# A fused decoder layer on one core: x's first quarter on ScalarE's queue, the small rows transposed after the first sums, and places of stored factors given back five half steps later

## The chip, the cores and the metric

The kernel runs on 1 core of one Trainium2 chip. The metric is the device time of that core in microseconds (us), the median of the runs of a kernel; lower is better. The engines are named as the profile names them: PE (TensorE), DVE (VectorE), ACT (ScalarE), POOL (GpSimd) and SP (SyncE, which here only issues transfers). "SPq" and "ACTq" are the queues on which SP and ACT issue transfers; an engine works its instructions off in the order in which they stand, issues of transfers included.

## The reference

One layer: a modulated RMS norm, one wide input projection, eight heads of stick-breaking attention, eight heads of chunkwise retention, an output projection with a gate and a residual. S = 1024 rows, D = 2048, head width 128, all float32.

```python
mod = silu(c) @ w_ada + b_ada                 # -> shift, scale, gate, 2048 each
h   = rms_norm(x, norm_gain) * (1 + scale) + shift
proj = h @ w_in                               # 2048 -> 8192: q k v z | q k v z
oa  = stick_breaking_attention(rms_norm(q) , rms_norm(k), v) * silu(z)
ob  = head_group_norm(chunkwise_retention(rotary(q), rotary(k), v)) * silu(z)
y   = concat(oa, ob) @ w_out
out = x + gate * y
```

## The kernel before

**Products in three passes.** Each float32 operand is cut into a high part (ACT copies it to float32r) and a low part (DVE subtracts the high part); a product is then three matmuls, high by high, high by low, low by high (`mm3`, lines 190 to 192; the trace shows them as L190, L192 and L191). Cuts of weights are made by `split` into a pool of four high and four low buffers (tiles `wh`, `wl`), cuts of kept factors by `split_to` or by `high` and `low`.

**Stages.** In a first stage (lines 765 to 808) one eighth of the projection's columns is multiplied chunk by chunk for the first 512 rows of x: for each of 16 chunks `p` of D, x is transposed by PE (tiles `xtp`, copied to `xT`), the modulation for two chunks at a time is summed by PE from w_ada (tiles `ada`, sums `accp`, copied to `acc`, turned into columns as `mod`, and made into `mods` by DVE), `make_h` makes `h_hi` and `h_lo` out of `xT` and `mods`, and seven products per chunk (tiles `first`) run with the cut pieces `wh_first`, `wl_first` of the weight rows `wr`. The first of them needs `mods`, which needs the transposed table `cols` of the small rows (norm_gain, b_ada and the head gains), loaded by five small transfers into `rows`, transposed by PE (`rows_ps`) and copied by DVE. A second stage does the same for the other 512 rows and makes, a few pieces at a time, the right factors of what follows.

**The groups.** From then on the rest of the projection runs as seven products of a Strassen-like scheme per group of columns, in `ORDER1` = (2, 7, 4, 1, 6, 5, 3) for group 0. Their right factors are, in the order of `RIGHT`, B11, B21, B22, T4, T1, T2, T3, each of eight chunks k and two parts (`B21h`, `B21l` and so on). `B21`, `T3`, `T4`, `B11` (`FIXED`) stay in SBUF for group 0 and are stored to DRAM as they are used; `B22`, `T1`, `T2` are stored when made and loaded back later. An "entry" is one (group, product, half hh, column block q); it has twelve matmuls and two half steps: `tick()` is called after every second chunk, counts `clock`, and runs what `later(n, fn)` put off by n half steps and up to two pieces from the list `background`.

**Places.** All large tiles live in 92 places of 256 KB (`Slots`, 128 partitions by 512 words). `get` takes the place that has been free longest, `put` appends one to the list of the free ones. A `put` happens when the last use has been written into the program, not when that use has run: whoever gets the place waits on the chip for the last reader of the tile before, which for a stored factor is the transfer that stores it.

**What sets the order.** PE's instructions run in the order in which the code is written. Those of the other engines are ordered by a scheduler by priority; `tc.high_priority(AHEAD)` moves a block forward. Eight semaphores (DMAHW0 to DMAHW7) are given in turn to the transfers of both queues: a transfer that gets one again waits at its issue until the transfer eight before it has landed.

The lines that matter: `load_xq(0)` loads the first quarter of x's columns for row blocks 0 to 3 (four transfers of 256 KB), line 736; the small rows are loaded and transposed on lines 139 to 155; `low(n, k)` on line 619 makes the low part, stores both parts and gives both places back:

```python
            else:
                store(n, k, hi, lo)
                put(hi, lo)
```

Of the kernel before, what the change touches and what calls it, by code (L numbers as in the profile page):

```python
# [36 lines left out]
NW = 4  # L37
CLASSES = {"dst": 14, "raw": 24, "ring": 24, "att": 30}
XQ_LOAD = {0: 2, 4: 1, 8: 3}
XQ_STAT = {1: 0, 4: 2, 7: 1, 10: 3}  # L40
X_LOAD = {5: (4,), 7: (5,), 9: (6,), 11: (7,)}
X_STAT = {8: (4,), 10: (5,), 12: (6,), 13: (7,)}
BIAS_LEAD = 12
# [13 lines left out]
class Slots:  # L57
# [31 lines left out]
    def put(self, *tiles):  # L89
        for t in tiles:  # L90
            _, i, cls = self.of.pop(id(t))
            self.used[cls] -= 1
            self.free.append(i)
# [3 lines left out]
def layer_kernel(ctx, tc, x, c, w_ada, b_ada, norm_gain, w_in, sb_q_gain, sb_k_gain, ret_norm_gain, w_out,  # L97
# [33 lines left out]
    c_sb = cons.tile([P, 16], F32, name="c_sb")  # L131
    nc.scalar.dma_start(c_sb, c.rearrange("o (p j) -> (o p) j", j=16))
    kdec = cons.tile([P, NH], F32, name="kdec")

    silu_c = cons.tile([P, 16], F32, name="silu_c")
    nc.scalar.activation(silu_c, c_sb, AF.Sigmoid)
# [7 lines left out]
    nc.scalar.dma_start(rows[48:49, 0:P], sb_q_gain)  # L144
    nc.scalar.dma_start(rows[49:50, 0:P], sb_k_gain)
    nc.scalar.dma_start(rows[50:58, 0:P], ret_norm_gain.rearrange("o (k p) -> (o k) p", p=P))
    rows_ps = ps.tile([P, P], F32, tag="C", name="rows_ps")
    nc.tensor.transpose(rows_ps, rows[:, 0:P], ident)
    nc.vector.tensor_copy(cols, rows_ps[:, 0:58])
    put(rows)  # L150
    gain_c = cols[:, 0:16]
    shift_b = cols[:, 16:32]
    qkg = cons.tile([P, 1], F32, name="qkg")
    nc.vector.tensor_scalar(qkg, cols[:, 48:49], cols[:, 49:50], 1.0 / math.sqrt(HD), op0=ALU.mult, op1=ALU.mult)
    ret_g = cols[:, 50:58]

    def rsqrt_guess(y, m):
# [45 lines left out]
    def later(n, fn):  # L203
        due.setdefault(clock[0] + n, []).append(fn)
# [5 lines left out]
    def tick():  # L210
        clock[0] += 1
        for fn in due.pop(clock[0], ()):
            fn()
        pump()
        stepped = False
        for task in list(tasks):
            task[1] -= 1
            if task[1] > 0 or stepped and one_step[0]:
                continue
            stepped = True  # L220
            try:
                task[1] = next(task[0])
            except StopIteration:
                tasks.remove(task)
        if background and len(slots.free) >= 3:
            some(background, 2)
        next_sum()

# [268 lines left out]
    shift = cons.tile([P, KC], F32, name="shift")  # L497
    qb = cons.tile([P, 2, NH], F32, name="qb")
    nc.vector.memset(qb, 0.0)
    xt, ada, xT = {}, {}, {}  # L500

    def load_x(t):
        for qt in (0, 2, 1, 3):
# [3 lines left out]
    def load_ada(cc):  # L507

        col = (D + CHUNKS1[cc] * 2 * P) if cc < 8 else CHUNKS[cc - 8] * 2 * P
        for g in range(8):  # L510
            ada[cc, g] = ar = get(f"ada_{cc}_{g}")
            nc.sync.dma_start(ar.rearrange("p (j n) -> p j n", n=2 * P),
                              ada_rows[:, 2 * g:2 * g + 2, col:col + 2 * P])
# [67 lines left out]

    mods = cons.tile([P, KC], F32, name="mods")
    scale_b1 = cons.tile([P, KC], F32, name="scale_b1")
    nc.vector.tensor_scalar(scale_b1, cols[:, 32:48], 1.0, None, op0=ALU.add)

    def ada_mod(cc, acc):

# [30 lines left out]
    def low(n, k):  # L618
        def fn():
            src, hi = facs[n, k], facs.pop((n, k, "hi"))  # L620
            lo = get(f"{n}l_{k}", None, F32R, borrow=True)
            nc.vector.tensor_tensor(lo, src, hi.bitcast(F32), op=ALU.subtract)
            if n != "B21":
                put(facs.pop((n, k)))
            if n in FIXED:
                fixed[n, k] = hi, lo
            else:
                store(n, k, hi, lo)
                put(hi, lo)
        return fn  # L630

    def factors(ks):
# [129 lines left out]
        nc.vector.tensor_copy(row, tp)  # L762
        return row

    load_ada(0)
    load_xq(0)
    ws = {0: start_w(0, 0)}
    for p in range(2):
        x_turn(p, 0, "pj", 4)
    sums = {0: ada_sums(0)}  # L770
    ws[1] = start_w(1, 0)
    load_ada(1)
    with tc.high_priority(AHEAD):
        ada_mod(0, sums.pop(0))
        make_h(0, 0)
    make_h(1, 0)
    rawz = {}
    for p in range(KC):
# [1097 lines left out]
```

## Time and profile before

| what | us |
|---|---|
| median of 3 runs | 1894.58 (1893.50 to 1895.37) |
| the profiled execution, its own time | 1895.06 |
| its span in the profile | 1893.3 |
| PE busy in the span | 1866.6 (99%) |
| ACT busy | 831.4 (44%) |
| DVE busy | 1338.0 (71%) |
| moved by the transfer engines | 541.04 MB, 286 GB/s over the span |

The rest of the profile is shown with the prediction. A row of the timeline reads: start, duration, engine, line, operation, written tile, read tiles, shape, count, and in brackets the idle time of the engine before it with what ended it. Rows of PEld are the loads of weights that go with each matmul. The span is shorter than the execution's time by 1.76 us, and the profiled execution lies 0.48 us above the median.

### The profile page before, as it was taken

How to read it: one execution, taken by the hardware profiler on the slowest of the kernel's cores; microseconds unless marked ns; L12 is line 12 of the kernel's file. 1: busy time of each engine (PE TensorE's matmuls, PEld its weight loads, DVE VectorE, ACT ScalarE, POOL GpSimd, SP SyncE). 2: the span in 40 equal slices, each digit the busy share in tenths (PEclk: the TensorE clock that was granted, in tenths of full speed). 3: DMA queues.
4: the chain of work that ended last, by engine and by line, in shares of the span. 5: the costliest groups of instructions: out<-in, count | busy, mean ns of one | idle time of the engine just before them, and what ended most of it. 6: DMA issues, size and time to landing. Idle time of an engine off the chain costs nothing.

```text
span 1893.3 us, 28871 instructions
## 1 busy us (share of the span) xinstructions
PE 1866.6 (99%) x9515; PEld 1537.2 (81%) x9515; DVE 1338.0 (71%) x2598; ACT 831.4 (44%) x1559; POOL 81.9 (4%) x278
## 2 busy tenths in 40 slices
PE   7999999999999999999999999999999999999998
PEld 4777778888888888888888888888888888888887
DVE  2568775666768777776778686976686656596669
ACT  3647752224544454435543554334334455342231
POOL 0000000000100010001010101000000000000000
PEclk9999999999999999999999999999999999999999
DMA  9969999997798789978997989999997963994594
GB/s 332 354 207 317 315 334 374 377 357 263 235 299 303 244 286 297 303 274 287 292 320 265 302 277 307 294 303 288 299 341 247 270 211 111 371 364 149 183 316 162
DMA packets 411827, 541.04 MB, mean 286 GB/s; under 512 B 34078, under 2 KB 207512, under 8 KB 411676
## 3 DMA queue, kind: packets, MB, share of 16 engines
q1 hardware_dynamic: 411288, 539.02, 86.6%
q8 instruction: 75, 1.23, 0.3%
q14 instruction: 76, 0.62, 0.1%
q10 hardware_dynamic: 388, 0.17, 0.0%
HBM read 453.03 MB, written 86.02 MB: 285 GB/s over the span
## 4 chain that ended last, share of the span: by engine, by line
PE 90%; DVE 4%; DMA 4%; issue 1%; ACT 1%; SPq 0%; DVEq 0%; ACTq 0%
PE pj L190 19%; PE pj L192 19%; PE pj L191 18%; PE y L191 4%; PE y L190 4%; PE y L192 4%; PE first L190 3%; PE first L191 2%; PE first L192 2%; PE accp L575 2%; PE tp_B L1196 1%; PE oT L192 1%; PE oT L190 1%; PE oT L191 1%; PE zp L190 1%; PE zp L192 1%
## 5 line engine op out<-in xcount | busy, mean ns | idle before, releaser
L179 DVE TENSOR_TENSOR wl<-A,wh 128x512 fp32r<-128x512 f32 x392 | 270.0, 689 | 249.5 <-ACT wh L177 225.1
L177 ACT ACTIVATE wh<-A 128x512 fp32r<-128x512 f32 x392 | 246.7, 629 | 378.7 <-PE pj L191 357.7
L393 ACT ACTIVATE c<-pj 128x512 f32<-128x512 f32 x112 | 66.6, 598 | 162.3 <-PE pj L192 149.2
L396 DVE TENSOR_TENSOR c<-pj,c 128x512 f32<-128x512 f32 x112 | 74.9, 686 | 59.7 <-PE pj L192 59.5
L300 DVE TENSOR_TENSOR A<-A,A 128x512 f32<-128x512 f32 x160 | 109.3, 688 | 1.7
L190 PE MATMUL first<-h_hi,wh_first 128*128 128x512 f32 x224 | 94.5, 422 | 1.6 <-ACT h_hi L605 1.6
L1176 DVE TENSOR_TENSOR_SCAN om<-om 128x128 f32<-128x128 f32 (+2 forms) x96 | 93.3, 972 | 1.1
L190 PE MATMUL pj<-T1h,wh 128*128 128x512 f32 x232 | 92.6, 399 | 0.0
L190 PE MATMUL pj<-B22h,wh 128*128 128x512 f32 x232 | 92.3, 398 | 0.0
L190 PE MATMUL pj<-B21h,wh 128*128 128x512 f32 x232 | 92.2, 398 | 0.0
L190 PE MATMUL pj<-B11h,wh 128*128 128x512 f32 x232 | 91.9, 396 | 0.0
L192 PE MATMUL pj<-B21h,wl 128*128 128x512 f32 x232 | 90.8, 391 | 0.0
L192 PE MATMUL pj<-T1h,wl 128*128 128x512 f32 x232 | 90.8, 391 | 0.0
L191 PE MATMUL pj<-B21l,wh 128*128 128x512 f32 x232 | 90.6, 391 | 0.0
L192 PE MATMUL pj<-B22h,wl 128*128 128x512 f32 x232 | 90.6, 391 | 0.0
L191 PE MATMUL pj<-T1l,wh 128*128 128x512 f32 x232 | 90.6, 390 | 0.0
L192 PE MATMUL pj<-B11h,wl 128*128 128x512 f32 x232 | 90.5, 390 | 0.0
L191 PE MATMUL pj<-B11l,wh 128*128 128x512 f32 x232 | 90.4, 390 | 0.0
L191 PE MATMUL pj<-B22l,wh 128*128 128x512 f32 x232 | 90.4, 390 | 0.0
L192 PE MATMUL pj<-T3h,wl 128*128 128x512 f32 x224 | 88.1, 393 | 1.9 <-DVE wl L179 1.9
L190 PE MATMUL pj<-T3h,wh 128*128 128x512 f32 x224 | 88.7, 396 | 0.8 <-ACT wh L177 0.8
L190 PE MATMUL pj<-T4h,wh 128*128 128x512 f32 x224 | 89.3, 399 | 0.0
(400 smaller groups left out, 4930.6 us busy)
## 6 DMA issues: line engine op xcount, KB each, us to landing
A<-in_w_in_dram SPq DMA_DIRECT2D x228, 256.0 KB, 5.7
ada<-in_w_ada_dram SPq DMA_DIRECT2D x128, 256.0 KB, 5.6
wB<-in_w_out_dram SPq DMA_DIRECT2D x112, 256.0 KB, 5.3
gr<-in_w_ada_dram SPq DMA_DIRECT2D x64, 256.0 KB, 5.7
T2h<-fac_T SPq DMA_DIRECT2D x56, 256.0 KB, 5.2
T2l<-fac_T SPq DMA_DIRECT2D x56, 256.0 KB, 5.4
T1h<-fac_T SPq DMA_DIRECT2D x56, 256.0 KB, 5.4
T1l<-fac_T SPq DMA_DIRECT2D x56, 256.0 KB, 5.4
```

The lines of the kernel that those rows point to most:

```text
L177: nc.scalar.activation(hi[:, 0:n], src[:, 0:n], AF.Copy)
L179: nc.vector.tensor_tensor(lo[:, 0:n], src[:, 0:n], hi[:, 0:n].bitcast(F32), op=ALU.subtract)
L190: nc.tensor.matmul(o, a_hi, b_hi, start=first, stop=False, skip_group_check=on)
L191: nc.tensor.matmul(o, a_hi, b_lo, start=False, stop=False, skip_group_check=on)
L192: nc.tensor.matmul(o, a_lo, b_hi, start=False, stop=last, skip_group_check=on)
L300: nc.vector.tensor_tensor(r[o], r[a], r[b], op=ALU.add if n == 1 else ALU.subtract)
L393: nc.scalar.activation(t, o, AF.Copy)
L396: nc.vector.tensor_tensor(dst[q, cc], o, dst[q, cc], op=ALU.add)
L575: nc.tensor.matmul(ap_[32 * g:32 * g + 32, :], silu_z[:, j, :], ada[cc, j // 2][:, (j % 2) * 256:(j % 2) * 256 + 256], start=j < 4, stop=j ...
L1176: nc.vector.tensor_tensor_scan(rev, rev, rev, init, op0=ALU.mult, op1=ALU.bypass)
L1196: nc.tensor.transpose(banks_[j // 2][:, c0:c0 + P], be[:, j * P:(j + 1) * P], ident)
```

## The change

The whole diff:

```diff
-XQ_STAT = {1: 0, 4: 2, 7: 1, 10: 3}
+XQ_STAT = {1: 0, 5: 2, 7: 1, 10: 3}
...
     kdec = cons.tile([P, NH], F32, name="kdec")
+    xt = {}
+    for t in range(4):
+        xt[t, 0] = get(f"x_{t}_0")
+        nc.scalar.dma_start(xt[t, 0], x2[t * P:(t + 1) * P, 0:HALF])
...
     nc.scalar.dma_start(rows[50:58, 0:P], ret_norm_gain.rearrange("o (k p) -> (o k) p", p=P))
-    rows_ps = ps.tile([P, P], F32, tag="C", name="rows_ps")
-    nc.tensor.transpose(rows_ps, rows[:, 0:P], ident)
-    nc.vector.tensor_copy(cols, rows_ps[:, 0:58])
-    put(rows)
...
-    nc.vector.tensor_scalar(qkg, cols[:, 48:49], cols[:, 49:50], 1.0 / math.sqrt(HD), op0=ALU.mult, op1=ALU.mult)
...
-        if background and len(slots.free) >= 3:
+        if background and len(slots.free) >= 4:
             some(background, 2)
...
-    xt, ada, xT = {}, {}, {}
+    ada, xT = {}, {}
...
-    nc.vector.tensor_scalar(scale_b1, cols[:, 32:48], 1.0, None, op0=ALU.add)
...
                 store(n, k, hi, lo)
-                put(hi, lo)
+                if clock[0]:
+                    later(5, lambda: put(hi, lo))
+                else:
+                    put(hi, lo)
...
-    load_ada(0)
-    load_xq(0)
-    ws = {0: start_w(0, 0)}
-    for p in range(2):
-        x_turn(p, 0, "pj", 4)
-    sums = {0: ada_sums(0)}
+    with tc.high_priority(AHEAD):
+        load_ada(0)
+        ws = {0: start_w(0, 0)}
+        for p in range(2):
+            x_turn(p, 0, "pj", 4)
+        sums = {0: ada_sums(0)}
+        rows_ps = ps.tile([P, P], F32, tag="B", name="rows_ps")
+        nc.tensor.transpose(rows_ps, rows[:, 0:P], ident)
+        nc.vector.tensor_copy(cols, rows_ps[:, 0:58])
+        put(rows)
+        nc.vector.tensor_scalar(qkg, cols[:, 48:49], cols[:, 49:50], 1.0 / math.sqrt(HD), op0=ALU.mult, op1=ALU.mult)
+        nc.vector.tensor_scalar(scale_b1, cols[:, 32:48], 1.0, None, op0=ALU.add)
+        ada_mod(0, sums.pop(0))
+        make_h(0, 0)
     ws[1] = start_w(1, 0)
     load_ada(1)
-    with tc.high_priority(AHEAD):
-        ada_mod(0, sums.pop(0))
-        make_h(0, 0)
     make_h(1, 0)
```

PE's order changes in one place only: `rows_ps`, its first instruction before, now stands between the last `accp` and the first `mod`. SP's list loses the four loads of x at the start, and in group 0 some stores change places. The other engines change as follows; the word in brackets names the semaphore that an instruction waits for.

ACT, at the very start, before (`c_sb` is the conditioning vector, `junk` the squares of x for the norm, `wr` and `wh_first` the first weights):

```order
L132 DMA c_sb<-in_c_dram 128x16
L142 DMA rows<-in_norm_gain_dram 16x128 [waits DVE_49]
L143 DMA rows<-in_b_ada_dram 32x128
L144 DMA rows<-in_sb_q_gain_dram 1x128
L145 DMA rows<-in_sb_k_gain_dram 1x128
L136 ACT_TABLE_LOAD
L136 ACTIVATE silu_c<-c_sb 128x16 [waits DMAHW0_49]
L146 DMA rows<-in_ret_norm_gain_dram 8x128 [waits DMAHW3_49]
```

The same place now:

```order
L137 DMA x_0_242<-in_x_dram 128x512
L137 DMA x_0_244<-in_x_dram 128x512
L137 DMA x_0_246<-in_x_dram 128x512 [waits DMAHW0_49]
L140 ACT_TABLE_LOAD
L140 ACTIVATE silu_c<-c_sb 128x16
L146 DMA rows<-in_norm_gain_dram 16x128 [waits DMAHW4_49,DVE_49]
L147 DMA rows<-in_b_ada_dram 32x128 [waits DMAHW6_49]
L148 DMA rows<-in_sb_q_gain_dram 1x128 [waits DMAHW7_49]
L149 DMA rows<-in_sb_k_gain_dram 1x128 [waits DMAHW1_49]
L150 DMA rows<-in_ret_norm_gain_dram 8x128 [waits DMAHW3_49]
L744 ACTIVATE junk_0_460,sq_268<-x_0_240 128x512 [waits DMAHW2_49]
L744 ACTIVATE junk_0_462,sq_268<-x_0_242 128x512
```

The small rows stood ahead of everything and did not wait for another transfer but for one; now each waits for a semaphore of a large one. Counted off in turn over both queues, DMAHW4 is then that of x's second piece, DMAHW6 of its third, DMAHW7, DMAHW1 and DMAHW3 those of the fourth, fifth and seventh piece of `ada`. Behind the last of them stand two squares, four conversions `wh_first` with `xT` among them, and two more squares ahead of the first `h_hi`.

DVE, at the start, before:

```order
L149 COPY cols<-rows_ps 128x58
L154 TENSOR_SCALAR qkg<-cols 128x1
L584 TENSOR_SCALAR scale_b_263<-cols 128x16
L560 COPY xT_0_310<-xtp_0_311 128x512
L179 TENSOR_TENSOR wl_first_0_0_297<-wr_0_0_291,wh_first_0_0_295 128x512
L179 TENSOR_TENSOR wl_first_0_1_301<-wr_0_1_293,wh_first_0_1_299 128x384
L579 COPY acc_334<-accp_317 128x256
L179 TENSOR_TENSOR wl_first_0_0_342<-wr_0_0_336,wh_first_0_0_340 128x512
L595 TENSOR_TENSOR mods<-mod_364,scale_b_263 128x2
L179 TENSOR_TENSOR wl_first_0_1_346<-wr_0_1_338,wh_first_0_1_344 128x384
L596 TENSOR_TENSOR mods<-mods,cols 128x2
```

And now:

```order
L559 COPY xT_0_305<-xtp_0_306 128x512
L178 TENSOR_TENSOR wl_first_0_0_292<-wr_0_0_286,wh_first_0_0_290 128x512
L178 TENSOR_TENSOR wl_first_0_1_296<-wr_0_1_288,wh_first_0_1_294 128x384
L178 TENSOR_TENSOR wl_first_0_0_351<-wr_0_0_345,wh_first_0_0_349 128x512
L178 TENSOR_TENSOR wl_first_0_1_355<-wr_0_1_347,wh_first_0_1_353 128x384
L578 COPY acc_329<-accp_312 128x256
L774 COPY cols<-rows_ps 128x58
L776 TENSOR_SCALAR qkg<-cols 128x1
L777 TENSOR_SCALAR scale_b_267<-cols 128x16
L593 TENSOR_TENSOR mods<-mod_336,scale_b_267 128x2
L594 TENSOR_TENSOR mods<-mods,cols 128x2
```

`acc` stood behind the two cuts of the first chunk's weights; now it stands behind all four, those of the second chunk too, and `cols` behind it.

ACT, in group 0, where product 2 ends and product 7 begins (`c` copies a finished bank of product 2, `wh_7_q_hh` is the high part of product 7's left factor, `B22h`, `T1h`, `B11h` are high parts of right factors), before:

```order
L615 ACTIVATE T1h_3153<-xT_1_2552 128x512 [waits DMAHW1_49]
L177 ACTIVATE wh_7_1_0_3161<-S_1_0_3093 128x512 [waits DVE_49,Activation_49]
L615 ACTIVATE B22h_3175<-xT_1_2639 128x512 [waits DMAHW3_49,DVE_49,Activation_49]
L393 ACTIVATE c_0_3_3183<-pj_2_3_3005 128x512 [waits DMAHW1_49,PE_49]
L615 ACTIVATE B22h_3189<-xT_1_2709 128x512 [waits DVE_49]
L177 ACTIVATE wh_7_2_0_3195<-S_2_0_3125 128x512
```

And now:

```order
L613 ACTIVATE T1h_3153<-xT_1_2552 128x512 [waits DMAHW1_49]
L176 ACTIVATE wh_7_1_0_3161<-S_1_0_3093 128x512 [waits DVE_49,Activation_49]
L392 ACTIVATE c_0_3_3177<-pj_2_3_3005 128x512 [waits DVE_49,PE_49,Activation_49]
L176 ACTIVATE wh_7_2_0_3183<-S_2_0_3125 128x512
L613 ACTIVATE B22h_3197<-xT_1_2639 128x512 [waits DMAHW5_49,PE_49]
L613 ACTIVATE B22h_3209<-xT_1_2709 128x512 [waits DMAHW7_49,PE_49]
```

`c_0_3` no longer waits for a transfer, and the two `B22h` stand behind `wh_7_2_0`. Counting the free list through the code: before, `c_0_3` gets the place of `T2h` of chunk 6, `T1l` of chunk 6 (DVE) that of `T2l` of chunk 6, and `S_0_1` (DVE, the left sum of product 7) that of `T2h` of chunk 7, all three still being stored. Now `c_0_3` gets the place of a factor that DVE has finished with, `S_0_1` that of `S_1_0`, and the stored parts' places go, five half steps later, to parts of B11: `B11l` of chunk 5 gets that of `T1h` of chunk 7, `B11h` of chunk 7 that of `B22h` of chunk 6. In those half steps the list of free places runs down to none (to 4 before). From half step 50 on each place goes to the same tile after the same tile as before.

## The prediction

> **What bounds the kernel now.** I read the page first, then a table of the whole span by stage, then the timeline where the table shows PE idle.
>
> ```profile
> span 1893.3 us, 28871 instructions
> PE 1866.6 (99%) x9515; PEld 1537.2 (81%) x9515; DVE 1338.0 (71%) x2598; ACT 831.4 (44%) x1559; POOL 81.9 (4%) x278
> ...
> 0.00:21.88 21.88, 7.79 (x45) 3.98 (x46) 5.11 (x18) 7.42 (x17) 0.70 (x6) 1.00 0.93 300
> 21.88:110.00 88.12, 88.12 (x573) 66.66 (x574) 45.16 (x145) 47.11 (x107) 0.00 (x0) 1.00 1.06 354
> 110.00:125.00 15.00, 15.00 (x98) 11.46 (x98) 7.95 (x21) 6.62 (x11) 0.00 (x0) 1.00 0.01 3
> ...
> 262.00:270.00 8.00, 5.35 (x20) 3.79 (x20) 3.50 (x6) 2.61 (x5) 0.00 (x0) 0.93 0.95 324
> 270.00:280.00 10.00, 10.00 (x40) 8.12 (x39) 10.00 (x18) 7.73 (x15) 0.00 (x0) 0.88 1.02 364
> ...
> 300.00:500.00 200.00, 200.00 (x932) 164.69 (x931) 127.07 (x220) 66.86 (x122) 6.00 (x24) 1.00 0.97 330
> ```
>
> The columns are PE, PEld, DVE, ACT and POOL busy with counts, then PE's clock, the transfers' share and GB/s. PE is the bound, idle for 1893.3 - 1866.6 = 26.7 us: 21.88 - 7.79 = 14.1 before the first product, 2.65 in 262 to 270, the rest in crumbs. The change touches just these two places. Between them PE never waits from 21.88 to 110, and the transfers end 15 us ahead of it (110 to 125: 3 GB/s): that stretch follows PE's start, not the loads. So a us gained at the start, or at 262, is kept, if no wait takes its place. After half step 50 nothing differs, neither order nor tenants of places; no row from 300 us on is expected to change but by the shift.
>
> **The start.** The order there says what is queued; these rows say how long.
>
> ```profile
> 4.51 0.28 ACTq L146 DMA_DIRECT2D rows<-in_ret_norm_gain_dram  x1
> 9.07 1.81 SPq L706 DMA_DIRECT2D wr<-in_w_in_dram  x4
> 12.42 0.48 PE L555 MATMUL xtp<-ident,x 128*128 128x128 f32 x1 [0.60 <-DMA x<-in_x_dram]
> 13.09 0.63 ACT L743 ACTIVATE junk<-x 128x512 f32<-128x512 f32 x1
> 13.11 0.48 PE L555 MATMUL xtp<-ident,x 128*128 128x128 f32 x1 [0.21 <-DMA x<-in_x_dram]
> 13.78 1.33 PE L555 MATMUL xtp<-ident,x 128*128 128x128 f32 x5 [0.19 <-DMA x<-in_x_dram]
> 14.38 0.58 ACT L562 ACTIVATE xT<-xtp 128x512 f32<-128x512 f32 x1
> 14.86 1.97 ACT L177 ACTIVATE wh_first<-wr 128x512 fp32r<-128x512 f32 x4
> 15.03 3.64 PE L575 MATMUL accp<-ada,silu_z 128*32 128x256 f32 x32
> 18.77 0.42 DVE L579 COPY acc<-accp 128x256 f32<-128x256 f32 x1 [1.87 <-PE accp L575]
> 20.30 0.16 DVE L595 TENSOR_TENSOR mods<-mod,scale_b 128x2 f32<-128x2 f32 x1 [0.51 <-PE mod L590]
> 20.38 0.56 DVE L179 TENSOR_TENSOR wl_first<-wr,wh_first 128x384 fp32r<-128x384 f32 x1
> 20.85 0.15 DVE L596 TENSOR_TENSOR mods<-mods,cols 128x2 f32<-128x2 f32 x1
> 21.88 0.80 PE L190 MATMUL first<-h_hi,wh_first 128*128 128x512 f32 x1 [1.62 <-ACT h_hi L605]
> 26.65 0.39 PE L192 MATMUL first<-h_hi,wl_first 128*128 128x512 f32 x1
> ```
>
> Now: ada lands, then x (last piece 13.78), eight transposes, 32 sums `accp` until 18.67, then `acc`, `mod`, `mods`, `h_hi`, first product. The change lets ada and x load side by side. The transfers are busy 93% of that window, so their sum lands when it did, at 13.8, only it is now ada's last piece and x is there earlier. The sums then run as pieces land and their last eighth ends 3.64 / 8 = 0.46 us later, at 14.3 instead of 18.7. That is 4.4 us, if nothing else were queued. But `acc` now stands on DVE behind all four `wl_first`, and these follow ACT's four conversions. ACT cannot start these until its last small row is issued, which waits for ada's seventh piece: 13.8 less one spacing of pieces (13.11 to 13.78, 0.7) = 13.1; with its issue, 0.28, 13.4. Two squares follow (13.09 to 14.38 for two now: 1.3), then four conversions and `xT` (1.97 + 0.48): 17.1. The weights themselves are no later: the last conversion began by 14.86 + 1.97 - 0.5 = 16.3, so all `wr` had landed, and the same bytes are ahead of them. The last `wl_first` ends 0.56 later, 17.65, where `acc` starts. From `acc` to the first product it takes 21.88 - 18.77 = 3.1 now, of which 0.4 goes because the last `wl_first` no longer stands between the two `mods` (20.85 against 20.30 + 0.16); `cols`, `qkg` and `scale_b`, moved there, run under PE's `mod`, and cost their durations, some 0.6, only if the small rows land after `acc`. So the first product starts at 17.65 + 2.7 = 20.35. **Gain 1.5 us.** Bounds: none, if the chain on ACT is 1.5 longer; 3.8, if the weights and ACT come earlier by as much as SP has fewer issues ahead of them (the four loads of x took 2.26 us there):
>
> ```profile
> 5.83 2.26 SPq L736 DMA_DIRECT2D x<-in_x_dram  x4
> 24.17 2.59 SPq L736 DMA_DIRECT2D x<-in_x_dram  x4
> 36.27 0.60 PE L555 MATMUL xtp<-ident,x 128*128 128x128 f32 x4
> ```
>
> I take 1.5, since every step of it has a row. The next thing late would be x's next quarter: issued until 26.8 and, at the same 5.7 from issue (13.78 less 8.1), landed at 32.5, needed at 36.27; 3.8 of cover, of which 1.5 is used. The square statistics of that quarter one chunk later (`XQ_STAT`) cost nothing: ACT is busy 47.11 of 88.12 there.
>
> The slow stretch behind the first product stays: the product at 21.88 takes 0.80, that at 26.65 0.39, which is what they take from there on; 4.8 us lie between, though the clock column reads 1.00. The Trainium skill, TensorE: Matmul & The Clock Gate, "What's actually happening", says that the array runs at half clock until it has been busy for about 3.4 us, by a window that runs free. By that rule the stretch could last 3.4 instead of 4.8, which at half pace is 0.7 us more gain (an estimate from that page): 1888.0 instead of the time below.
>
> **The stall at 262.** The chain of waits passes through a store here.
>
> ```profile
> L190 PE MATMUL pj<-T3h,wh x32: 389/389/632, 259.6 to 285.4; 128*128 128x512 f32 x32
> L190 PE MATMUL pj<-T4h,wh x32: 389/389/389, 286.1 to 307.2; 128*128 128x512 f32 x32
> L190 PE MATMUL pj<-B11h,wh x7: 389/389/389, 307.9 to 312.0; 128*128 128x512 f32 x7
> ...
> 264.25 0.60 ACT L393 ACTIVATE c<-pj 128x512 f32<-128x512 f32 x1 [7.78 <-DMA fac_T<-T2h]
> 264.92 0.69 DVE L622 TENSOR_TENSOR T1l<-xT,T1h 128x512 fp32r<-128x512 f32 x1 [7.43 <-DMA fac_T<-T2l]
> 267.20 0.69 DVE L360 TENSOR_TENSOR S<-A,A 128x512 f32<-128x512 f32 x1 [1.58 <-DMA fac_T<-T2h]
> 268.54 0.50 PE L192 MATMUL pj<-T3h,wl 128*128 128x512 f32 x1 [1.87 <-DVE wl L179]
> ...
> 262.24 4.84 DMA fac_T<-T2h
> ...
> 241.66 8.12 SPq L264 DMA_DIRECT2D A<-in_w_in_dram  x10
> 258.43 1.67 SPq L366 DMA_DIRECT2D fac_T<-T2h  x1
> 262.24 0.64 SPq L366 DMA_DIRECT2D fac_T<-T2h  x1
> 272.24 0.75 SPq L366 DMA_DIRECT2D fac_T<-T3h  x1
> 276.99 0.75 SPq L367 DMA_DIRECT2D fac_T<-T3l  x1
> ```
>
> Product 7 (T3) and product 4 (T4) have 96 matmuls each. T3 takes 286.1 - 259.6 = 26.5, T4 307.9 - 286.1 = 21.8: **4.7 us lost**, slow products behind the idle included (granted clock 0.93 and 0.88). `c` and `T1l` wait 7.8 and 7.4 us for places whose tenants are being stored, `wh` and `wl` of product 7 queue behind them. With the change `c` waits only for its product, which ends at 259.6 less one entry, 2.7 (21.8 / 8): 256.9. `wh_7_2_0` follows by 258.2 and is needed at 259.6 + 5.4 = 265. So this stall goes whole.
>
> What is late next: `B11l` of chunk 5 on DVE waits for the store of `T1h` of chunk 7, and the last `wl` of product 7 stands behind it. In the new order this store is 14 transfers behind what was issued at 262.24; at 0.68 each (272.24 to 276.99 in seven) that is 271.8, and landing takes 4.84 (the chain's own piece, before `S` is let go) to 5.8 (258.43 to 264.25): 276.6 to 277.6. `B11l` and `wl`, 0.69 each: 278.0 to 279.0. PE needs this `wl` at 259.6 + 7 x 2.72 + 0.45 = 279.05. Likewise `B11h` of chunk 7 on ACT waits for the store of `B22h` two transfers on, 278.0 to 279.0; it, two copies and `wh` of product 4 (some 2.2 in all, at the 0.5 to 0.6 apiece of ACT's conversions) end at 280.2 to 281.2; needed at 259.6 + 21.8 = 281.4. Both just fit. I charge 0.3; at the 0.81 of the loads of A (8.12 / 10) it would be 1.7 to 2. **Gain 4.4**, bounds 2.7 and 4.7. Giving places back later and asking for four free ones costs only that: the pieces they hold back are parts of B11, wanted from 307.9 on.
>
> **Sum.** 1895.06 - 1.5 - 4.4 = 1889.2 for an execution like the profiled one; this lies 0.48 above the median of the runs, so 1888.7.
>
> **Rivals.**
> *The start gives nothing:* ACT's chain of waiting small rows and squares ends 1.5 later than I have it. For it: each small row now waits for a large transfer, and ACT's order has no way round them. Against: the bytes are the same. 1894.6 - 4.4 = 1890.2. The Trainium skill, DMA: Bandwidth & Descriptors, "Issuing engines are not separate DMA queues", says that issuing from a second engine saves only the time of the issues; by that rule this rival would be the likelier one for what the loads give, and no run yet shows it.
> *The stall comes back at the next store:* the store of `T1h` lands some 2 to 3 us later than I reckon, DVE stands, and PE waits for the last `wl` of product 7. For it: a cover of 0 to 1 us; against: transfers at 0.68 apiece in that stretch. Gain 1.5 + 2 = 3.5: 1891.1.
> *The free list does not do what I counted:* only the start gains: 1893.1.
> *Slower:* SP's loads of ada and `wr` for the second chunks now wait, eight transfers on, for the small rows on ACT's queue. Should the last small row land only near 21, SP's loads stop and the transfers run dry; x's next quarter then lands after PE needs it. Its cover is 3.8 - 1.5; the loss counts one for one from there, and from 8 us of standstill (2.3 + 5.9) the kernel is slower; at 10, 1896.4. Against: five rows of a few KB.
>
> **How the numbers follow.** The forecast 0.60, the start for nothing 0.16, the stall back 0.15, the miscount 0.04, slower 0.05. A measurement of this kernel can tell about 0.2%, 3.8 us, from no change. Faster by more: the forecast, two thirds of the first rival and a few of the second, 0.74; within: 0.21; slower 0.05. The range goes from 1894.6 - 3.8 - 4.7 = 1886.1 to the second rival and part of the third, 1892.4.
>
> **What would show it.** `acc` starting at 17 to 18.5 straight behind a `wl_first`, the first product at 20 to 20.7; `c` in group 0 running within 1 us of its product, no idle PE between 262 and 270, T3's 96 products in under 22.5 us; and `B11l` waiting some 5 us for the store of `T1h`. PE waiting for `wl` at the end of T3 shows the second rival, waits of `xtp` or `wh_first` for loads in 25 to 40 us the last. A first product after 21.9 would prove the start wrong.

## The result, and the profile after

| kernel | median, us | runs | its profiled execution: time / span |
|---|---|---|---|
| before, beside it | 1893.66 (1892.94 to 1895.63) | 8 | 1895.06 / 1893.3 |
| changed | 1888.64 (1888.12 to 1889.36) | 8 | 1889.35 / 1887.6 |

The ratio is 0.9971, with a 95% interval of 0.9962 to 0.9981: 5.0 us faster, where 5.9 was predicted and 1888.7 stood against the 1888.64 measured. The head of the changed kernel's page:

```profile
span 1887.6 us, 28872 instructions
PE 1864.6 (99%) x9515; PEld 1536.4 (81%) x9515; DVE 1339.3 (71%) x2598; ACT 831.3 (44%) x1559; POOL 82.0 (4%) x278
```

Its table by stage, with the columns of the one shown of before:

```profile
0.00:20.25 20.25, 7.32 (x46) 3.58 (x46) 5.25 (x18) 7.21 (x17) 0.70 (x6) 0.99 0.84 266
20.25:110.00 89.75, 89.75 (x578) 67.89 (x578) 46.29 (x149) 47.59 (x108) 0.00 (x0) 0.96 1.07 360
262.00:270.00 8.00, 8.00 (x37) 6.63 (x36) 8.00 (x14) 4.57 (x9) 0.00 (x0) 1.00 1.08 365
270.00:280.00 10.00, 10.00 (x46) 8.29 (x45) 3.62 (x6) 3.31 (x7) 0.00 (x0) 1.00 1.05 371
```

PE is busy 2.0 us less in a span that is 5.7 shorter; it no longer stands in 262 to 270, and the clock there reads 1.00 where it read 0.93 and 0.88. New is the 0.96 behind the first product; in the kernel before the column reads 1.00 there, but its products were slow as well until 26.65 (the last section says why the column misses that). The timeline of the start:

```profile
12.13 3.64 PE L574 MATMUL accp<-ada,silu_z 128*32 128x256 f32 x32
13.17 0.31 ACTq L150 DMA_DIRECT2D rows<-in_ret_norm_gain_dram  x1
14.77 0.61 ACT L176 ACTIVATE wh_first<-wr 128x512 fp32r<-128x512 f32 x1
15.77 1.47 ACT L176 ACTIVATE wh_first<-wr 128x384 fp32r<-128x384 f32 x3
16.31 1.68 DVE L178 TENSOR_TENSOR wl_first<-wr,wh_first 128x384 fp32r<-128x384 f32 x3 [0.20 <-ACT wh_first L176]
17.91 0.42 DVE L578 COPY acc<-accp 128x256 f32<-128x256 f32 x1
18.38 0.61 PE L588 MATMUL mod<-ones,acc 128*128 128x1 f32 x4 [2.20 <-DVE acc L578]
20.25 0.79 PE L189 MATMUL first<-h_hi,wh_first 128*128 128x512 f32 x1 [1.26 <-ACT h_hi L603]
26.32 0.59 PE L191 MATMUL first<-h_hi,wl_first 128*128 128x512 f32 x1
26.75 0.39 PE L189 MATMUL first<-h_hi,wh_first 128*128 128x512 f32 x1
```

The first product starts 1.63 earlier than in the profile of before, but products reach 0.39 only at 26.75, where it was 26.65: the slow stretch lasts 6.5 us instead of 4.8. Group 0 by tile:

```profile
L189 PE MATMUL pj<-T3h,wh x32: 389/389/389, 258.6 to 279.7; 128*128 128x512 f32 x32
L189 PE MATMUL pj<-T4h,wh x32: 389/389/389, 280.4 to 301.4; 128*128 128x512 f32 x32
```

and by the timeline:

```profile
256.14 0.60 ACT L392 ACTIVATE c<-pj 128x512 f32<-128x512 f32 x1 [1.13 <-issue]
270.89 0.71 SPq L365 DMA_DIRECT2D fac_T<-T1h  x1
275.88 0.69 DVE L620 TENSOR_TENSOR B11l<-xT,B11h 128x512 fp32r<-128x512 f32 x1 [5.54 <-DMA fac_T<-T1h]
277.14 0.63 ACT L613 ACTIVATE B11h<-xT 128x512 fp32r<-128x512 f32 x1 [6.69 <-DMA fac_B<-B22h]
```

T3's first product comes 1.0 earlier (259.6 before), its 96 products take 280.4 - 258.6 = 21.8 instead of 26.5. From T4 to the end nothing moved: 1887.6 - 280.4 = 1607.2, and 1893.3 - 286.1 = 1607.2. So the 5.7 of the span are 4.7 in group 0 and 1.0 at the start.

### The profile page after: what moved, and what is told of

Read it like the earlier page. It is cut to its first block, busy times and chain, and to the rows that moved or that the text cites. A ratio compares the mean times of both kernels' runs of the same rounds, so it can differ in the third digit from the quotient of the medians.

```text
span 1887.6 us, 28872 instructions
## 1 busy us (share of the span) xinstructions
PE 1864.6 (99%) x9515; PEld 1536.4 (81%) x9515; DVE 1339.3 (71%) x2598; ACT 831.3 (44%) x1559; POOL 82.0 (4%) x278
## 4 chain that ended last, share of the span: by engine, by line
PE 93%; DVE 5%; DMA 1%; issue 1%; ACT 1%; ACTq 0%; SPq 0%; DVEq 0%
PE pj L189 19%; PE pj L191 19%; PE pj L190 19%; PE y L191 5%; PE y L190 5%; PE y L189 5%; PE first L189 3%; PE first L190 3%; PE first L191 3%; PE accp L574 1%; PE tp_B L1202 1%; PE oT L191 1%; PE oT L189 1%; PE oT L190 1%; PE zp L190 1%; PE zp L191 1%
## 5 line engine op out<-in xcount | busy, mean ns | idle before, releaser
L189 PE MATMUL pj<-T2h,wh 128*128 128x512 f32 x224 | 89.1, 398 | 0.0
L191 PE MATMUL first<-h_hi,wl_first 128*128 128x512 f32 x224 | 88.8, 396 | 0.0
## 6 DMA issues: line engine op xcount, KB each, us to landing
A<-in_w_in_dram SPq DMA_DIRECT2D x228, 256.0 KB, 5.7
ada<-in_w_ada_dram SPq DMA_DIRECT2D x128, 256.0 KB, 5.7
wB<-in_w_out_dram SPq DMA_DIRECT2D x112, 256.0 KB, 5.4
gr<-in_w_ada_dram SPq DMA_DIRECT2D x64, 256.0 KB, 5.6
T2h<-fac_T SPq DMA_DIRECT2D x56, 256.0 KB, 5.4
T2l<-fac_T SPq DMA_DIRECT2D x56, 256.0 KB, 5.4
T1h<-fac_T SPq DMA_DIRECT2D x56, 256.0 KB, 5.4
T1l<-fac_T SPq DMA_DIRECT2D x56, 256.0 KB, 5.3
```

What stands on the lines that cost most here:

```text
L189: nc.tensor.matmul(o, a_hi, b_hi, start=first, stop=False, skip_group_check=on)
L191: nc.tensor.matmul(o, a_lo, b_hi, start=False, stop=last, skip_group_check=on)
```

## The experiments

Each ratio is to the kernel before, run in the same rounds.

| run | median, us | ratio, 95% interval | first product | products at 0.42 or less from | T3's first product | T3's 96 products |
|---|---|---|---|---|---|---|
| before (profile) | | | 21.88 | 26.65 | 259.6 | 26.5 |
| changed | 1888.64 | 0.9971 (0.9962 to 0.9981) | 20.25 | 26.75 | 258.6 | 21.8 |
| start_only | 1893.75 | 0.9997 (0.9988 to 1.0006) | 21.04 | 26.24 | 258.3 | 26.5 |
| put_only | 1889.83 | 0.9978 (0.9968 to 0.9987) | 20.46 | 26.85 | 258.7 | 21.7 |
| put_again | 1889.58 | 0.9976 (0.9967 to 0.9985) | 21.03 | 24.50 | 257.7 | 21.8 |
| after_again | 1888.98 | 0.9974 (0.9965 to 0.9983) | 19.81 | 25.89 | 257.9 | 21.8 |
| later1 | 1892.69 | 0.9991 (0.9983 to 1.0000) | 20.14 | 25.79 | 257.7 | 25.0 |
| later2 | 1891.58 | 0.9985 (0.9976 to 0.9994) | 19.75 | 25.82 | 257.8 | 24.5 |
| ada_first | 1887.22 | 0.9964 (0.9952 to 0.9977) | 18.75 | 23.42 | 256.0 | 21.7 |
| rows_pool | 1888.09 | 0.9969 (0.9957 to 0.9981) | 19.28 | 24.93 | 257.2 | 21.8 |
| warm | 1887.85 | 0.9967 (0.9954 to 0.9979) | 20.13 | 24.83 | 257.0 | 21.7 |
| warm2 | 1887.87 | 0.9967 (0.9955 to 0.9980) | 19.93 | 24.45 | 256.5 | 21.8 |
| best1 | 1886.34 | 0.9959 (0.9946 to 0.9971) | 19.21 | 20.34 | 256.2 | 21.8 |
| best2 | 1884.91 | 0.9951 (0.9938 to 0.9963) | 18.61 | 19.73 | 254.1 | 21.8 |

### The two parts apart

start_only is the change with places free at once and three asked for:

```diff
-                if clock[0]:
-                    later(5, lambda: put(hi, lo))
-                else:
-                    put(hi, lo)
+                put(hi, lo)
...
-        if background and len(slots.free) >= 4:
+        if background and len(slots.free) >= 3:
```

> Only the start of the change: x's first quarter on ScalarE's queue, the small rows transposed behind the sums, one square statistic a chunk later; places are counted free at once and three free ones suffice, as before. Theory A (the two parts add up): first product near 20.3 us as in the changed kernel, a slow stretch of 6.5 us behind it, so that the first product of T3 starts 1.0 earlier than the 259.6 of before, and the stall of T3 is all there (its 96 products in 26.5): 1.0 us faster than before, 1892.6 beside a median of 1893.66. Rival B (the stall goes with the start, because the loads run further ahead of PE): T3's 96 products in 22 to 24 us, 1888 to 1890. Rival C (the start alone gives its whole 1.6): 1892.0.

put_only is the reverse: the kernel before, with only these lines of the change in it.

> Only the other part: the kernel before, with places of stored right factors counted free five half steps behind the store, and four free places asked for. Theory A: first product at 21.9 as before, T3's 96 products in 21.8 instead of 26.5, c running within about 1 us of its product: 4.7 us faster than before, 1889.0. Rival B (the stall needs the earlier start too): a part of the stall stays, T3's 96 products in 23 to 26 us, 1890 to 1893. Rival D (the new waits for the stores of T1h and B22h, covered with 1 to 3 us in the changed kernel, are not covered with the start 1.6 later): PE waits at the end of T3 or the head of T4, 1889.5 to 1891.

T3's first rows by tile, of start_only and then of put_again, which is put_only run once more:

```profile
L189 PE MATMUL pj<-T3h,wh x32: 389/389/628, 258.3 to 284.1; 128*128 128x512 f32 x32
L189 PE MATMUL pj<-T4h,wh x32: 389/389/389, 284.8 to 305.9; 128*128 128x512 f32 x32
```

```profile
L190 PE MATMUL pj<-T3h,wh x32: 389/389/389, 257.7 to 278.8; 128*128 128x512 f32 x32
L190 PE MATMUL pj<-T4h,wh x32: 389/389/389, 279.5 to 300.6; 128*128 128x512 f32 x32
```

With the start alone the stall is all there (the slowest product 628 ns, T3 26.5 us); with the places alone it is gone. So the stall belongs to the places (theory A; rival B of each run falls), and the new waits do no harm with the later start either (rival D falls). In time the places are worth 3.9 (1893.74 to 1889.83; theory A of put_only had 4.7), and 4.5 in the later rounds; the start is worth 0.0 in start_only, where 1.0 was expected, and its first product came at 21.04 instead of near 20.3. To see whether that zero holds, the changed kernel and put_only ran once more side by side:

> The changed kernel once more, timed on the same chip and in the same rounds as put_again, for what the start's part is worth on top of the other. Theory A (the start is worth about half of what the first product gains, since the slow stretch behind it takes the rest, and its place shifts from one execution to the next): 0.3 to 1.3 us faster than put_again. Rival B (the start is worth nothing, as the run start_only, 1893.75 beside 1893.74, had it): within 0.3 us of put_again. Rival C (it is worth the whole 1.5 of the prediction): 1.4 to 1.7.

> The other part alone once more (as the run put_only), beside after_again. Theory A: 0.3 to 1.3 us slower than after_again, T3's 96 products in 21.8 us again. Its first product, with the order of before, came at 20.46 in put_only and at 21.88 in the profile of before: if the same order gives another such pair here, a us and more of the difference between two profiles of the start is the execution's, not the change's.

after_again is 0.6 faster than put_again, inside what the intervals leave open (0.9965 to 0.9983 against 0.9967 to 0.9985). The table shows why the start is hard to weigh. One and the same order of the start gave a first product at 21.88, 20.46 and 21.03 (before, put_only, put_again), the other at 20.25, 21.04, 19.81, 20.14 and 19.75 (changed, start_only, after_again, later1, later2). The means, 21.12 and 20.20, are 0.9 apart; those of T3's first product, 258.67 and 258.06, 0.6. So of the first product's 0.9 some two thirds are kept, as far as three and five executions can tell, and one execution can be a us off either way. Theory A of after_again fits best; rival B, no gain at all, isn't excluded by the times.

In the order of before that spread is PE's pace and nothing else. The sums `accp` start at 15.03 in the profile of before and at 15.04 in put_only and put_again; they take 3.64, 2.62 and 3.18 us, and `mod` behind them takes 1.01, 0.61 and 0.61. These differences, 1.42 and 0.86, are the whole distance of the first products (21.88 beside 20.46 and 21.03). The sums of put_only:

```profile
15.04 2.62 PE L575 MATMUL accp<-ada,silu_z 128*32 128x256 f32 x32
```

So the profile that the prediction started from was one in which PE ran at the slow pace up to the first product and past it.

### How long a place has to stay taken

later1 and later2 are the change with a shorter delay:

```diff
-                    later(5, lambda: put(hi, lo))
+                    later(1, lambda: put(hi, lo))
```

> The changed kernel with places counted free one half step behind the store instead of five. By the order of places, c of group 0 then no longer takes the place of T2h of chunk 6, but T1l of chunk 6 does (before it took that of T2l), and the difference S of product 7 takes the place of T2h of chunk 7, as it did in the kernel before. Theory A (a stall is where a tenant whose store is not through is taken by work in front of PE's next factors; S's wait for T2h until 267.2 alone held the last factor of product 7): the stall stays though c runs on time: T3's 96 products in 25 to 26.5 us, 3.2 to 4.7 slower than the changed kernel, 1891.8 to 1893.3. Rival B (c's late run on ScalarE is the cause, T1l's and S's waits are beside it): T3's 96 products in 21.8 to 23, 1888.6 to 1889.8. Rival C (the length of the delay does not matter, only that four places are asked for): as the changed kernel, 1888.6.

> The changed kernel with places counted free two half steps behind the store instead of five. By the order of places T1l and T2l of chunks 6 and 7 then take places that are not being stored, loads of A take that of T2h, and S of product 7 takes the place of T2l of chunk 6, whose store was through at 264.9 in the kernel before. Theory A: S runs at 264.9 instead of 267.2 and the last factor of product 7 stands ready at 266.2, where PE would want it at 264.5 to 265.5: T3's 96 products in 22 to 23.5 us, 0.3 to 1.7 slower than the changed kernel, 1889.0 to 1890.3. Rival B (two half steps suffice): 21.8, and 1888.6. Rival C (the whole delay of five is needed, since loads of A that wait for T2h's store hold up SP's queue and the stores behind them): 24 us or more, 1891 and above.

The timeline of later1:

```profile
265.03 0.69 DVE L359 TENSOR_TENSOR S<-A,A 128x512 f32<-128x512 f32 x1 [2.27 <-DMA fac_T<-T2h]
266.38 0.50 PE L191 MATMUL pj<-T3h,wl 128*128 128x512 f32 x1 [1.70 <-DVE wl L178]
```

and its T3 by tile:

```profile
L189 PE MATMUL pj<-T3h,wh x32: 389/389/499, 257.7 to 282.0; 128*128 128x512 f32 x32
```

`c` ran on time there, and still `S` waits for T2h's store and PE for the `wl` behind it: T3 takes 25.0, 3.2 more than with the whole delay, and the time is 1892.69. So `c`'s lateness was not the cause by itself; what stalls PE is whatever stands ahead of its next factor and takes a place that is being stored (theory A of later1; its rivals fall).

later2 is slower than theory A had it (1891.58 against at most 1890.3) and comes out as rival C said, 24 us and more. Its table by stage:

```profile
262.00:270.00 8.00, 7.59 (x33) 5.64 (x32) 7.09 (x12) 5.76 (x11) 0.00 (x0) 1.00 0.99 342
270.00:280.00 10.00, 8.85 (x39) 6.70 (x38) 5.91 (x11) 3.21 (x7) 0.00 (x0) 1.00 1.00 339
```

The chain of waits through that stretch (start, duration, what):

```profile
256.38 5.83 DMA fac_T<-T2h
...
262.22 4.30 DMA A<-in_w_in_dram
...
275.01 3.43 DMA fac_B<-B22l
```

And its timeline where PE waits the second time:

```profile
277.50 0.63 ACT L613 ACTIVATE B11h<-xT 128x512 fp32r<-128x512 f32 x1 [6.79 <-DMA fac_B<-B22h]
278.53 0.69 DVE L620 TENSOR_TENSOR B11l<-xT,B11h 128x512 fp32r<-128x512 f32 x1 [4.09 <-DMA fac_B<-B22l]
278.70 0.50 PE L189 MATMUL pj<-T3h,wh 128*128 128x512 f32 x1 [0.71 <-ACT wh L176]
```

By the chain a load of A waits on SP's queue for T2h's store, 256.38 to 262.2, and lands at 266.5 with a `wl` behind it; the stores queued behind that load wait with it. PE idles only 0.41 by 270, but `B11h` and `B11l`, waiting for the stores of `B22h` and `B22l`, now do hold it up from 278 on: 1.15 idle. This second stall is like the prediction's rival "the stall comes back at the next store", but behind B22's stores and not T1h's, and smaller: by the starts of T3's products, which are 0.23 apart where nothing waits, it costs some 1.7 us of the 2.7 that T3 takes longer, where the rival had 2.4. Two half steps are 2.7 us and five 6.8 (an entry of two takes 2.7), and T1h's store takes 5.0 from issue to landing (270.89 to 275.88, above): of the two only the longer delay covers it. The 3 and 4 between weren't tried.

### What sets the first product

ada_first puts the second chunk's weights behind its ada on SP's queue; with that their conversions fall behind `h_hi` on ACT, and `acc` stands behind two `wl_first` instead of four:

```diff
-    ws[1] = start_w(1, 0)
     load_ada(1)
+    ws[1] = start_w(1, 0)
```

> The changed kernel, with the eight loads of ada for the second chunks ahead of the weights of the second chunk on SP's queue; the order follows it: the conversions wh_first of the second chunk go behind h_hi on ScalarE, and acc stands behind two wl_first instead of four on VectorE. Theory A (the first product is set by VectorE's order, acc behind the second chunk's wl_first): acc starts at 16.8 to 17.0 instead of 17.91, the first product at 19.1 to 19.5 instead of 20.25; what is kept of that is 0.5 to 1.0 us: 1887.7 to 1888.2 beside 1888.64 of the changed kernel. Rival B (the sums or the rows set it: accp's end, 15.77, and the row transposes until 16.18 are the bound): under 0.3 us. Rival C (the second chunk's weights, now eight loads later, come too late for PE): wh_first of that chunk after 26 and PE waits for it, slower than the changed kernel by 1 us or more.

rows_pool issues the small rows from POOL (in all five loads of `rows`):

```diff
-    nc.scalar.dma_start(rows[0:16, 0:P], ...
+    nc.gpsimd.dma_start(rows[0:16, 0:P], ...
```

> The changed kernel with its five loads of small rows issued from GpSimd's queue instead of ScalarE's. Theory A (the chain of the prediction: ScalarE stands from the fourth load of x until its last small row is issued at 13.17, so the squares and the conversions wh_first start at 13.53): the squares run as x lands, from 6.5 to 11.5, wh_first starts when its weights land, 0.5 to 1.5 earlier; the last wl_first and with it acc move from 17.91 to 16.5 to 17.4, no earlier than the weights of the second chunk allow (in the run start_only wh_first waited 0.77 us for them until 16.84); the first product at 19.0 to 19.8. What is kept of it hangs on where the clock rises, 0.3 to 2.0 us: 1886.6 to 1888.3 beside 1888.64. Rival B (the weights' landing binds): acc stays within 0.4 of 17.9, no difference. Rival C (SP's loads come to stand behind the small rows on the new queue too): SP's loads of ada and weights pause, the transfers run dry for over 1 us before 30, slower by up to 1 us.

The timeline of ada_first, then of rows_pool:

```profile
16.01 0.42 DVE L578 COPY acc<-accp 128x256 f32<-128x256 f32 x1
18.75 0.80 PE L189 MATMUL first<-h_hi,wh_first 128*128 128x512 f32 x1 [1.26 <-ACT h_hi L603]
...
23.12 0.47 PE L190 MATMUL first<-h_lo,wh_first 128*128 128x512 f32 x1
23.42 0.40 PE L191 MATMUL first<-h_hi,wl_first 128*128 128x512 f32 x1
```

```profile
13.99 1.04 ACT L176 ACTIVATE wh_first<-wr 128x512 fp32r<-128x512 f32 x2 [2.68 <-DMA wr<-in_w_in_dram]
14.66 2.36 DVE L178 TENSOR_TENSOR wl_first<-wr,wh_first 128x512 fp32r<-128x512 f32 x4 [2.48 <-ACT wh_first L176]
16.93 0.42 DVE L578 COPY acc<-accp 128x256 f32<-128x256 f32 x1
```

Both links of the predicted chain are real. Without the two extra `wl_first`, `acc` starts at 16.01 instead of 17.91, straight behind the second one, and the first product at 18.75: 1.4 us of time (theory A, and more than its 0.5 to 1.0), though the two intervals overlap, and its slow stretch of 4.7 us beside 6.5 may have a share in it. Without the small rows on ACT the conversions start at 13.99 instead of 14.77, and then it is the weights' landing they wait for; the first product comes at 19.28. Its time, 0.55 less, lies within what the measurement can't tell.

### The slow stretch behind the first product

warm and warm2 are the change with products that nobody reads (their counts: five and two, eleven and seven); best1 is ada_first with five and seven, best2 the same with six and seven and the rows on POOL:

```diff
+        warm = ps.tile([P, HALF], F32, tag="A0", bufs=1, name="warm")
+        w00 = ws[0][0][0]
+        for _ in range(5):
+            nc.tensor.matmul(warm[:, 0:256], w00[:, 0:P], w00[:, 0:256], start=True, stop=True)
         ada_mod(0, sums.pop(0))
+        for _ in range(2):
+            nc.tensor.matmul(warm[:, 0:256], w00[:, 0:P], w00[:, 0:256], start=True, stop=True)
         make_h(0, 0)
```

> The changed kernel with seven extra products of 128x256, whose result nobody reads, on PE: five between the row transpose (ends 16.18) and mod (18.38), two between mod and the first product (20.25). Theory A (the slow stretch behind the first product, 20.25 to 26.75, is the price of PE's idle time ahead of it: 16.18 to 18.38 and 19.0 to 20.25): with PE kept busy from 12.13 on, products run at 0.39 from 20.25 or within 1 us of it, and the time falls by 2 to 3 us, to 1885.6 to 1886.6. Rival B (the stretch is counted from the first of the large products, whatever ran ahead): it stays at 6.5 behind 20.25, and the time is that of the changed kernel, 1888.6, or 0.5 more if mod or the first product stand behind the extra ones. Rival C (the stretch ends at a set point of time near 26.7, as it did in both kernels at 26.65 and 26.75): its end stays at 26.7 and the time too; then an earlier first product gains at half pace only.

> The changed kernel with eighteen extra products of 128x256, eleven ahead of mod and seven between mod and the first product, and the loads in the changed kernel's order. In the run warm, five and two left PE idle for 2.0 us ahead of mod, the clock fell at 17.9 and rose at 24.7. Theory A (only a stretch of some 3.4 us without a standstill keeps the clock up): with the gap ahead of mod filled to 0.3 to 1.0 us the clock stays up in most executions and is up at the first product: 1.0 to 2.3 us faster than the changed kernel, 1886.4 to 1887.6. Rival B (what best1 gained over the changed kernel, 2.3, came from the order of loads alone): no faster than warm, 1887.8 to 1888.6. Rival D (eleven products at the slow pace, 2.3 us, hold up mod): the first product 0.3 to 0.6 later, 1888 to 1889.

> The changed kernel with ada of the second chunks loaded ahead of the second chunk's weights (as in the run ada_first) and twelve extra products of 128x256 whose result nobody reads: five between the row transpose and mod, seven between mod and the first product. In ada_first PE stood still there for 0.7 and 1.3 us. Theory A (the granted clock rises at the end of a stretch of some 3.4 us in which PE never stood still, these stretches follow one another wherever the kernel is: the clock fell at 19.9 and rose at 26.7 in the changed kernel, 6.8 apart, and in the runs start_only, put_only and warm too): PE is busy from 10.5 on without a gap over 0.3 us, so the clock is up before the first product near 18.8; products run at 0.39 from the first on; 4.7 us of slow stretch at some half pace go, 1.7 to 2.3 us: 1885.0 to 1885.5 beside 1887.22 of ada_first. Rival B (only the large products raise the clock): slow behind the first product for 3.4 to 6.8 us, 1887 to 1887.7. Rival D (the extra products stand in the way): mod or the first product 0.5 to 1 later, 1887.5 to 1888.

> As best1, with the small rows issued from GpSimd's queue and one extra product of 128x256 more ahead of mod. Theory A (ScalarE's squares then run as x lands, and the first conversion starts when its weights land, 0.3 to 0.9 before the 14.86 of best1): the first product 0.3 to 0.9 earlier, still at 0.39 to 0.5 a piece, 1885.5 to 1886.1 beside 1886.34 of best1. Rival B (the weights' landing and the sums bind, as in rows_pool, where the first conversion waited 2.68 for its weights): no difference, 1886.2 to 1886.5.

The table by slices of half a us, whose third column from the end is the granted clock, of the changed kernel and then of put_again:

```profile
19.50:20.00 0.50, 0.00 (x0) 0.00 (x0) 0.00 (x0) 0.50 (x1) 0.00 (x0) 0.91 1.07 344
20.00:20.50 0.50, 0.25 (x1) 0.26 (x1) 0.27 (x1) 0.50 (x2) 0.00 (x0) 0.50 1.00 326
26.50:27.00 0.50, 0.50 (x4) 0.36 (x3) 0.00 (x0) 0.44 (x1) 0.00 (x0) 0.77 1.09 346
```

```profile
20.00:20.50 0.50, 0.00 (x0) 0.00 (x0) 0.16 (x2) 0.24 (x1) 0.00 (x0) 1.00 1.11 354
21.00:21.50 0.50, 0.47 (x1) 0.29 (x1) 0.49 (x1) 0.50 (x1) 0.00 (x0) 0.53 1.08 368
24.00:24.50 0.50, 0.50 (x2) 0.35 (x2) 0.00 (x0) 0.50 (x1) 0.00 (x0) 0.56 1.08 344
```

The clock is either 1.00 or 0.50, so a mean tells where in its slice it changed. In the changed kernel it fell at 19.91 (0.91 is 0.41 us of 1.00 and 0.09 of 0.50) and rose at 26.73: 6.82 apart. In put_again it fell at 21.03, just as the first product began, and rose at 24.44: 3.41. In warm (17.87 to 24.70) and rows_pool (18.13 to 24.95) it is 6.83 and 6.82 by the same reckoning. So the clock changes on a beat of 3.41 us, which lies at another place in the kernel from one execution to the next, and each of these rises came at the end of a beat in which PE was busy throughout. start_only bears the beat out far from the start: its clock fell twice, at 19.38 and, where PE stood in T3, at 268.55.

```profile
19.00:19.50 0.50, 0.45 (x4) 0.46 (x4) 0.41 (x3) 0.10 (x2) 0.00 (x0) 0.88 1.02 340
268.50:269.00 0.50, 0.50 (x3) 0.40 (x2) 0.50 (x2) 0.50 (x2) 0.00 (x0) 0.55 0.92 340
```

The 249.17 between them are 73 beats of 3.413. A first product that just misses a beat's start waits nearly two beats, one that comes with it one: the 1.63 won in the changed profile brought no earlier rise than the profile of before had, and 0.6 of it went again; in ada_first, 18.75 was early enough for a rise near 23.4. The Trainium skill, TensorE: Matmul & The Clock Gate, "What's actually happening", gives this beat as a window of 3413 ns that runs free of the kernel; by that, 3.41 and 6.82 are one and two windows, and the traces agree.

Whether filling PE's gaps ahead of the first product keeps the clock up is what the four runs with extra products tell. In warm a gap of 1.98 ahead of `mod` was left and the clock fell: 1887.85, not the 1885.6 to 1886.6 of theory A; nor did its rivals hold, for the stretch ended at 24.83, 4.7 us behind the first product. In warm2 the first product ran in 0.50, but then the clock fell at 21.06 and rose at 24.47; the beat before that fall held gaps of some 1.0 us in all (0.42 of the 0.88 ahead of `mod`, 0.33, 0.28). It gained 1.1 on after_again, just short of theory A's range and inside that of rival B (no faster than warm), so the times don't tell these two apart. best2 by the timeline:

```profile
14.52 1.05 ACT L176 ACTIVATE wh_first<-wr 128x512 fp32r<-128x512 f32 x2 [2.60 <-DMA wr<-in_w_in_dram]
16.26 0.42 DVE L578 COPY acc<-accp 128x256 f32<-128x256 f32 x1
16.73 0.61 PE L588 MATMUL mod<-ones,acc 128*128 128x1 f32 x4 [0.43 <-DVE acc L578]
17.20 1.07 PE L784 MATMUL warm<-wh_first 128*128 128x256 f32 x7
18.61 0.49 PE L189 MATMUL first<-h_hi,wh_first 128*128 128x512 f32 x1 [0.33 <-ACT h_hi L603]
19.39 0.50 PE L190 MATMUL first<-h_lo,wh_first 128*128 128x512 f32 x1 [0.29 <-DVE h_lo L605]
20.64 0.40 PE L190 MATMUL first<-h_lo,wh_first 128*128 128x512 f32 x1
```

No slow stretch is left in the one profile of best1 or of best2, as theory A of best1 had it; its rival B falls by the profile. Rival D comes near in what it foretold (`mod` 0.86 and the first product 0.46 later than in ada_first), but its reason doesn't hold: the extra products ended at 17.21, ahead of `mod`, which started 0.47 behind `acc` as in ada_first; `acc` itself came 0.86 later, as did the last small row's issue (13.29 beside 12.43). best1's time, 1886.34, stayed 0.8 above theory A's range: PE idled 0.67 in 27 to 60 us (32.33 busy of 33), about half of it for a load of x, and the kernel before took 0.4 more in these rounds than in ada_first's. In these profiles T3 starts no earlier in best1 (256.2) than in ada_first (256.0), and the intervals of their times overlap: what the extra products are worth by themselves isn't shown.

best2 had 33.00 of 33.00 busy in 27 to 60 and is the fastest, 1884.91: 9.2 us below before and 4.1 below after_again, both in the same rounds, and its interval lies clear of after_again's. How its three differences (order of loads, rows on POOL, extra products) share the 4.1 stays open. The range expected of best2 (1885.5 to 1886.1) was too high: the first product, 18.61, came 0.6 earlier as theory A said, though the conversions again waited for their weights; T3 came 2.1 earlier than in best1. Of the other 1.5, best1's idle time makes 0.67 at 27 to 60 and 0.26 at 122 to 200; the rest wasn't followed up.

## Why the prediction was right, point by point

- **The stall at 262, 4.4 of 4.7.** Right, and whole: T3's 96 products 21.8, no idle PE, `c` at 256.14 (256.9 foretold). The 0.3 charged for new waits was not needed. `B11l` waited 5.54 for T1h's store, issued at 270.89 (271.8 foretold) and landed by 275.88 (276.6 to 277.6); `B11h` waited for `B22h` until 277.14, about 1 us ahead of what was reckoned. In time the places are worth 3.9 to 4.5. That the cover was thin was right too: later2 lost it.
- **The start, the first product at 20.35.** 20.25. Its chain was the one named: last small row issued at 13.17 (13.1 foretold), the conversions and `xT` done at 17.24 (17.1), `acc` straight behind a `wl_first` at 17.91 (17.65), and 2.34 from there to the first product (2.7; `mod` took 0.61 instead of 1.01). One step failed without effect: the sums do not run as ada's pieces land and end at 14.3; PE reaches them only behind its transposes, at 12.13, and they take 3.64 in one block, to 15.77. `acc` was late on DVE anyway.
- **The start's gain, 1.5, kept whole.** The term that was too large: by the means of the profiles 0.9 at the first product and 0.6 at T3; by the times 0.0 in start_only and 0.6 in after_again. Two steps of it failed. The 21.88 it was counted against is the latest of three executions of that order, by 0.8 over their mean, because PE ran its `accp` and `mod` at the slow pace; and "a us gained at the start is kept" and "the slow stretch stays" hold only if the clock rises earlier with PE, which it does in steps of 3.41. The window of the Trainium skill was weighed there as a stretch of 3.4 that could only give more. Since the beat runs free of the kernel, a first product that misses its start has nearly two beats ahead of it, and this execution had (6.5).
- **From the profiled execution to the median.** 0.48 was taken off; beside medians of 1893.7 to 1894.1 the profiled 1895.06 lay 0.9 to 1.4 above. That puts the forecast's start 0.5 to 0.9 too high, and with the start's 0.9 too much gain the two cancel: 1888.7 and 1888.64 agree better than their terms.
- **The rivals.** "The start gives nothing" is nearer than its chance of 0.16 suggests: 0.6 stands between 0 and 1.5, but not by its mechanism, since ACT's chain ended on time (17.24). The Trainium skill's rule named there, DMA: Bandwidth & Descriptors, "Issuing engines are not separate DMA queues", isn't contradicted: the last small row's issue waited for ada until 13.17, as if the sum of the bytes had landed no earlier. The miscount and the dried-up transfers did not happen (360 GB/s from 20.25 to 110, and PE did not wait for x's next quarter).
- **The idle time called crumbs.** Of the 10 us that the prediction left over, 5.3 are the end of the span, from PE's last product near 1888.0 to 1893.3. It bears on no term of the sum.

## What to carry to other kernels

A place that is being stored is not free: if the allocator can hand it out again before the store has landed, look what stands behind the taker on its engine, and delay its return by the store's whole way (here 5 us, under a delay of 6.8), not by a step or two. Weigh a gain of a us or two ahead of a row of products against several executions, not one profile; it moves in steps with the clock's beat. Filling PE's gaps before it took the slow stretch out of two profiles; whether it is worth more than the earlier start isn't shown here. When one piece of work on a queue waits, reckon the next wait with everything behind it shifted too.

## What the runs showed of the hardware

- The granted clock of PE changes only on a beat of 3.41 us and between 1.00 and 0.50 (above); the same order of instructions had slow stretches of 3.5 (put_again) and 6.4 us (put_only).
- About 1.0 us of gaps, none over 0.42 within the beat, let it fall in warm2, though PE was busy for 70% of that beat; in warm2's beat before that one, 14.24 to 17.65, 0.53 and 0.46 did not (`mod` behind it took 0.61), nor did 1.05 us of gaps between 16.3 and 19.4 in best2 (0.43, 0.33, 0.29). How much a beat bears, and how the gaps lay to the beat in best2, stays open.
- The clock column reads 1.00 ahead of the first change in a trace whatever the pace: ada_first shows 1.00 throughout its start, and its products take 0.80 and 0.63 until 23.12. The durations tell the truth there.
